# Last layer's second feed-forward product: channels on the partitions before, tokens on the partitions after

## The chip, the cores and the metric

One Trainium2 chip, one of its cores, one launch. The metric is device time in microseconds (us) of the whole program. Before the change the median of three timed runs is 2346.48 us (2346.24 to 2348.11).

## What is computed

A backbone of two layers over 256 latent tokens with 256 context tokens ahead of them, 1024 channels wide. Each layer mixes the tokens in three branches (a state-space scan, grouped attention, differential attention), adds the result to the stream and normalises it, and then runs a gated feed-forward product of inner width 2816 and normalises again. In the last layer only the latent tokens are wanted (`need_ctx` is false). What the change touches is the end of that layer:

```python
def swiglu(h, w_in, w_out):
    a, b = jnp.split(h @ w_in, 2, axis=-1)
    return (jax.nn.silu(a) * b) @ w_out
...
x = layer_norm(DEEPNORM_ALPHA * x + mod_l[5][:, None]
               * swiglu(modulate(x, mod_l[3], mod_l[4]), ffn_w_in[i], ffn_w_out[i]),
               ln2_g[i], ln2_b[i])
...
return x
```

`mod_l` is a row of six times 1024 modulation values, made from the condition vector by one product with `ada_w[i]` (1024 x 6144) and the bias `ada_b[i]`; its sixth part, `mod_l[5]`, is the gate of the feed-forward product.

## The kernel before

The program is not run in the order in which it is written. `trunk` calls a recorder (`Plan`), which notes each instruction with its tiles; `Plan.schedule` then orders all of it with a list schedule for the whole program. It has a price for each instruction (`Plan.cost`), slots for the tiles of each class (`SIZES`: 65 buffers of 128x512 in class `s2`, 15 of 128x1024 for weights in `w4`, 8 PSUM banks in `ps`), and a priority that says when TensorE, never idle, would want a result. So a change of a price or of a tile's life can move instructions anywhere in the program. All instructions are emitted from one line (L586 before, L585 after); in the trace, groups are told apart by tile names and shapes: `s` is a 128x512 buffer, `shared` a part of one, `w` a weight tile, `ps` a PSUM bank, `cst` and `id` constants, `tiny` small columns, `misc` parameter columns.

fp32 weights are split on chip: ScalarE copies the rounded high part (type fp32r), VectorE subtracts to get the low part (`load_w`). A product is then three fp32r matmuls, high x high, high x low and low x high (`dense`, `mm3`). Products that stay in fp32 run in two records each in the trace; transposes run in one.

The end of the last layer before the change, in the order of recording:

- `w_o` product, 8 blocks of 128 channels; its result plus the residual `xa` goes to `rt`. Then `make_ada(i, range(10, 12))`: the product for the last two blocks of modulation values, 16 matmuls that run four side by side on strips of the array (a strip operation), then a copy, four transposes and a reduction to columns.
- `segment`: the layer norm of `rt` (`layer_norm`, channels on the partitions, so the sums over channels are products with a block of ones) and the next stream `hT`. `late` writes the residual for the next norm to DRAM (`xd1`), in steps during the first blocks; `load_xa` reads it back.
- Feed-forward: 22 blocks of 128 inner channels in three batches (8, 8, 6). A block is two products of 24 matmuls with 256 columns (`psd` banks, at most six), then sigmoid, two multiplications and `split` into `hh`, `hl`. After each batch the second product: for each of 8 blocks of output channels one load of `ffn_w_out` (128 x 1024, or 768 in the last batch) and 24 (18) matmuls with 256 columns (the tokens), then `resid`, which multiplies by the gate and adds to `rt2`.
- `layer_norm` of `rt2`, eight multiplications and activations with scale and bias, 16 transposes back to token rows, four copies, four loads of 256 KB to `out`.

PE, VectorE (DVE) and ScalarE (ACT) take their instructions in emitted order. Loads go out on SyncE's queue (SP), some on GpSimd's (POOL).

Of the kernel before, what the change touches and what calls it, by code (L numbers as in the profile page):

```python
# [10 lines left out]
F32R = mybir.dt.float32r  # L11
AF = mybir.ActivationFunctionType
ALU = mybir.AluOpType
# [31 lines left out]
LAST_ADA = 2  # L45
# [31 lines left out]
class View:  # L77
    """A slice of a planned tile: which part of it (for dependencies) and how to reach it."""
# [108 lines left out]
class Plan:  # L187
    """Records the program, then orders it with a list schedule that knows the on-chip memory."""
# [19 lines left out]
    def cost(self, eng, fn, out, ins, kw):  # L208
# [3 lines left out]
        if eng == "PE":  # L212
            if fn == "transpose":
                return 109
            rhs, m = ins[1], ins[0].shape[-1]
            n = self.free(rhs)
            if rhs.dt() == F32R:
                return max(n / 2.4 if n >= 256 else 4 * n / 2.4, 107) + 2.5
            return 2 * max(2 * n / 2.4, 107) + 4
        if eng == "DVE":  # L220
# [3 lines left out]
            if fn == "tensor_reduce":  # L224
# [89 lines left out]
    def schedule(self):  # L314
        """The best of some rounds: after each, what the tensor engine waited for gets a higher priority."""
# [30 lines left out]
    def round(self, bump):  # L346
# [13 lines left out]
        # priority: when the tensor engine, never idle, would want the result, and not long after the program's order  # L360
# [47 lines left out]
        def place(b):  # L408
            """The slot (and the part of it) that a tile goes to: one in part use before an empty one."""
# [197 lines left out]
def trunk(tc, x, c, cx, c_ctx, ada_w, ada_b, w_in, b_gate, conv_w, conv_b, dt_bias, a_log, ssm_d, norm_w,  # L607
# [42 lines left out]
    def load_w(src, kt, cols, step=0):  # L650
# [3 lines left out]
        if step:  # L654
            # columns in the order (halves, axes) instead of (axes, halves)
# [121 lines left out]

    def ada_parts(i, ccs, tag="aw"):
        """Modulation columns of some blocks of 512: each block has rows of its own in every strip of one sum."""
# [3 lines left out]
        for m, cc in enumerate(ccs):  # L783
            for k0 in (0, 4):
                ws = [t2(tag=tag, cap=CAP[tag]) for _ in range(4)]
                for g in range(4):
                    S.dma_start(out=ws[g], in_=ada_w[i][(k0 + g) * 128:(k0 + g + 1) * 128, cc * 512:(cc + 1) * 512])
                with plan.strips():
                    for g in range(4):
                        T.matmul(ps[32 * g:32 * g + 32, :], scT[:, k0 + g, 30 - 2 * m:62 - 2 * m], ws[g],  # L790
# [819 lines left out]
```

## Time and profile before

| what | value |
|---|---|
| median of the timed runs | 2346.48 us |
| span of the profiled execution (the program on the core, first to last instruction) | 2345.3 us |
| PE busy | 2301.0 us, 98% of the span |
| VectorE, ScalarE busy | 1670.1 us (71%), 1422.4 us (61%) |
| DMA, mean over the span | 158 GB/s |

No other time of the profiled execution is given; the median of the runs lies 1.2 us over its span. How to read it: PE is the engine that the others serve. A stretch in which PE is busy throughout lasts as long as its matmuls take; where it is not, something else sets the time. PE's busy time is made of modelled ends, so the pace of matmuls is taken from their count in a stretch.

### The profile page before, as it was taken

What the parts mean: (1) busy time and instruction counts of PE and PEld (TensorE: products, weight loads), DVE (VectorE), ACT (ScalarE), POOL (GpSimd) and SP (SyncE); (2) the same over time, 40 slices, a digit from 0 to 9 for tenths busy, and PEclk for the clock granted to TensorE, in tenths of its full rate; (3) what the DMA queues carried; (4) which work ended last, traced back from release to release, by engine and by line L of the source; (5) the groups of instructions that cost most, each with busy time, mean ns of one, the idle gap of its engine ahead of it and who ended that gap; (6) DMA issues with size and microseconds to landing.
All of it is one profiled execution on the core that took longest, in us unless ns stands there. A gap on an engine that the chain in (4) does not pass through costs nothing. (4 is left out here: it accounts for less than half of the span.)

```text
span 2345.3 us, 38903 instructions
## 1 busy us (share of the span) xinstructions
PE 2301.0 (98%) x14423; PEld 1940.3 (83%) x14423; DVE 1670.1 (71%) x3438; ACT 1422.4 (61%) x2887; POOL 135.1 (6%) x216
## 2 busy tenths in 40 slices
PE   8999999999999999999999999999999999999998
PEld 4877777887887788898777778989988798998997
DVE  3889857888988864476333337999698888767655
ACT  4778745867767753345323235888586676646554
POOL 3102102000100100000000000001010100000000
PEclk9999999999999999999999999999999999999998
DMA  9746544332433465576555425527443345798662
GB/s 332 214 135 175 181 132 135 102 112 72 133 104 98 133 216 175 184 219 213 171 163 168 139 74 151 150 76 217 132 129 114 105 126 164 214 274 240 191 188 66
DMA packets 520702, 370.37 MB, mean 158 GB/s; under 512 B 20706, under 2 KB 472674, under 8 KB 520512
## 3 DMA queue, kind: packets, MB, share of 16 engines
q1 hardware_dynamic: 507296, 329.63, 47.3%
q0 software_dynamic: 13216, 38.25, 5.5%
q8 instruction: 113, 1.85, 0.3%
q14 instruction: 77, 0.63, 0.1%
HBM read 334.00 MB, written 33.82 MB: 157 GB/s over the span
## 5 line engine op out<-in xcount | busy, mean ns | idle before, releaser
L586 PE MATMUL ps<-s,w 128*128 128x512 f32 (+2 forms) x7608 | 1524.0, 355 | 8.2 <-DVE s L586 4.6
L586 PEld LDWEIGHTS ps<-s,w 128*128 128x128 f32 (+1 forms) x7608 | 1236.0, 189 | 237.1 <-issue 28.8
L586 ACT CAST w<-w 128x1024 fp32r<-128x1024 f32 (+2 forms) x486 | 454.4, 944 | 486.3 <-DVE w L586 256.8
L586 DVE TENSOR_TENSOR w<-w,w 128x1024 fp32r<-128x1024 f32 (+2 forms) x486 | 528.0, 1092 | 299.8 <-PE ps L586 203.0
L586 PE MATMUL ps<-shared,w 128*128 128x256 f32 x2544 | 313.2, 283 | 0.0
L586 PE MATMUL ps<-s,s 128*64 128x128 f32 (+6 forms) x2320 | 303.2, 361 | 7.6 <-DVE s L586 2.1
L586 PEld LDWEIGHTS ps<-shared,w 128*128 128x128 f32 x2544 | 308.5, 192 | 0.5 <-issue 0.3
L586 ACT ACTIVATE s<-s 128x512 f32<-128x512 f32 x424 | 260.6, 630 | 31.0 <-DVE s L586 24.7
L586 PEld LDWEIGHTS ps<-s,s 128*64 128x64 f32 (+3 forms) x2320 | 186.9, 152 | 90.6 <-issue 31.9
L586 DVE TENSOR_TENSOR s<-s,s 128x512 f32<-128x512 f32 (+2 forms) x298 | 196.2, 674 | 36.7 <-ACT s L586 34.5
L586 DVE TENSOR_TENSOR s<-s,ps 128x512 f32<-128x512 f32 x116 | 79.1, 684 | 133.3 <-PE ps L586 65.7
L586 DVE SCALAR_TENSOR_TENSOR s<-ps,misc,s 128x510 f32<-128x510 f32 (+2 forms) x188 | 139.3, 741 | 13.9 <-ACT s L586 11.8
L586 PE MATMUL ps<-w,s 128*128 128x256 f32 x960 | 119.7, 284 | 0.0
L586 PEld LDWEIGHTS ps<-w,s 128*128 128x128 f32 x960 | 117.2, 192 | 2.2 <-issue 1.5
L586 DVE TENSOR_TENSOR shared<-shared,shared 128x256 f32<-128x256 f32 (+2 forms) x241 | 97.2, 417 | 24.4 <-ACT shared L586 22.6
L586 DVE TENSOR_TENSOR s<-ps,s 128x256 fp32r<-128x256 f32 (+1 forms) x204 | 85.6, 444 | 30.4 <-ACT s L586 25.7
L586 ACT ACTIVATE shared<-shared 128x256 f32<-128x256 f32 x232 | 92.4, 416 | 23.4 <-DVE shared L586 20.7
L586 ACT CAST s<-ps 128x256 fp32r<-128x256 f32 (+1 forms) x204 | 74.4, 396 | 36.0 <-PE ps L586 32.1
L586 ACT ACTIVATE s<-ps,misc 128x512 f32<-128x512 f32 x68 | 50.6, 744 | 73.2 <-PE ps L586 73.0
L586 POOL DMA_DIRECT2D s<-dram x96 | 71.9, 753 | 375.0 <-PE ps L586 274.7
L586 ACT ACTIVATE s<-ps,tiny 128x512 f32<-128x512 f32 x112 | 76.7, 689 | 26.5 <-DVE tiny L586 18.9
L586 DVE SCALAR_TENSOR_TENSOR shared<-ps,misc,shared 128x256 f32<-128x256 f32 (+2 forms) x144 | 67.2, 478 | 29.4 <-PE ps L586 20.4
(102 smaller groups left out, 1512.5 us busy)
## 6 DMA issues: line engine op xcount, KB each, us to landing
w<-in_w_in_dram SPq DMA_DIRECT2D x200, 512.0 KB, 4.0
s<-in_ada_w_dram SPq DMA_DIRECT2D x192, 256.0 KB, 4.9
w<-in_ffn_w_in_dram SPq DMA_DIRECT2D x88, 512.0 KB, 3.9
s<-dram POOLq DMA_DIRECT2D x96, 256.0 KB, 5.6
s<-dram SPq DMA_DIRECT2D x64, 256.0 KB, 4.1
w<-in_w_ssm_out_dram SPq DMA_DIRECT2D x32, 512.0 KB, 4.1
w<-in_ffn_w_out_dram SPq DMA_DIRECT2D x32, 512.0 KB, 3.9
shared<-dram SPq DMA_DIRECT2D x112, 128.0 KB, 3.9
```

The costliest lines, as they stand in the source:

```text
L586: getattr(attr[op.eng], fn)(*[real(v) for v in args], **{a: real(v) for a, v in kw.items()})
```

## The change

The last layer gets a second half of its own, `last_ffn`; the loop with three batches stays for the first layer alone.

- The second product is turned round: 128 tokens of `hh` or `hl` are the stationary operand and 512 output channels of `ffn_w_out` rows the moving one. Four PSUM banks (two halves of the tokens, two halves of the channels) collect the whole product from block 0 to block 21. Each block is multiplied as soon as it is made, those of blocks 18 to 21 together at the end, first all of token half 0, then all of token half 1.
- The gate is needed as rows in place of columns: `gate_rows` runs the same strip product, copies it, and with two fp32 matmuls by a selecting matrix puts the sums on all partitions, where the bias (a row loaded to all partitions) is added. The four transposes and the reduction go.
- The residual is turned to token rows on chip (`token_resids`, 16 transposes, in `xres`) in place of the way through DRAM.
- The norm works along the free dimension with `bn_stats` and `bn_aggr`; `ln2_g` and `ln2_b` are loaded as rows to all partitions, four loads of 256 KB on POOL's queue beside two for the bias. The final transposes go.
- `Plan.cost` prices an fp32r matmul anew. `LAST_ADA` is gone with the same value, 2, written out. Comments in the code go too.

```diff
             if rhs.dt() == F32R:
-                return max(n / 2.4 if n >= 256 else 4 * n / 2.4, 107) + 2.5
+                return (n if n >= 256 else 4 * n) / 2.4 + m / 9.6
...
+            def token_resids():
+                for q in range(2):
+                    xo = []
+                    for d in range(4 * q, 4 * q + 4):
+                        xo.append(t1())
+                        V.tensor_tensor(xo[-1], rt[d, 256], rss[0][1], ALU.mult)
+                        A.activation(xo[-1], xo[-1], AF.Identity, scale=ac[:, 0, d:d + 1], bias=ac[:, 1, d:d + 1])
+                    yield
+                    for t in range(2):
+                        ps = psum()
+                        for j in range(4):
+                            transpose(ps[:, j * 128:(j + 1) * 128], xo[j][:, t * 128:(t + 1) * 128])
+                        xres[t, q] = t2()
+                        A.copy(xres[t, q], ps)
+                    yield
...
+        def gate_rows():
+            bias = []
+            for m in range(2):
+                bias.append(t2())
+                src = ada_b[i][5 * D + m * 512:5 * D + m * 512 + 512]
+                G.dma_start(out=bias[m], in_=src.unsqueeze(0).to_broadcast([128, 512]))
+            ps = psum("ada", CAP["ada"])
+            for m in range(2):
+                for _ in ada_terms(i, ps, m, 10 + m, m == 0, m == 1):
+                    pass
+            ev = t2()
+            A.copy(ev, ps)
+            for m in range(2):
...
+                psg = psum()
+                T.matmul(psg, sel, ev, start=True, stop=True)
+                V.tensor_tensor(bias[m], bias[m], psg, ALU.add)
+            return bias
+
+        def last_ffn(grow):
+            outs = {(t, q): psum() for t in range(2) for q in range(2)}
+            waiting = []
+            for j in range(22):
...
+                split(hh, hl, sg)
+                wh, wl = load_w(ffn_w_out[i][j * 128:(j + 1) * 128, :], 1, D)
+                for t in range(2):
+                    waiting.append((t, j, hh, hl, wh, wl))
+                if j < 18 or j == 21:
+                    waiting.sort(key=lambda v: v[0])
+                    for t, n, hh, hl, wh, wl in waiting:
+                        ts_ = slice(t * 128, t * 128 + 128)
+                        for q in range(2):
+                            qs = slice(q * 512, q * 512 + 512)
+                            mm3(outs[t, q], hh[:, ts_], hl[:, ts_], wh[:, 0, qs], wl[:, 0, qs], n == 0, n == 21)
+                    waiting = []
...
+            for t in range(2):
+                st, mv, rs = tiny(12), tiny(2), tiny(1)
+                for q in range(2):
+                    r = xres[t, q]
+                    gated = t2()
+                    V.tensor_tensor(gated, outs[t, q], grow[q], ALU.mult)
+                    V.tensor_tensor(r, r, gated, ALU.add)
+                    V.bn_stats(out=st[:, 6 * q:6 * q + 6], in_=r)
+                V.bn_aggr(out=mv, in_=st.rearrange("p (c s) -> p c s", s=6))
+                rsqrt(rs, mv[:, 1:2], 1)
+                for q in range(2):
+                    r = xres[t, q]
+                    V.scalar_tensor_tensor(r, r, mv[:, 0:1], gb[0, q], ALU.subtract, ALU.mult)
+                    V.scalar_tensor_tensor(r, r, rs, gb[1, q], ALU.mult, ALU.add)
+                    S.dma_start(out=out[0, t * 128:(t + 1) * 128, q * 512:(q + 1) * 512], in_=r)
...
-            if i > 0 and LAST_ADA:
-                make_ada(i, range(12 - LAST_ADA, 12))
+            if not need_ctx:
+                grow = gate_rows()
             segment(t0, r)
```

The order moves everywhere in the program; three places matter below. A row names the written tile, the tiles read and the size of the result.

PE, second product of the last layer. Before, the end of one block of 128 output channels in the last batch (`ps_24818`), with 256 tokens as columns:

```order
L586 MATMUL ps_24818<-shared_3_24717,w_4703_24704 128x256 x2
L586 MATMUL ps_24818<-shared_28_24361,w_4704_24715 128x256
L586 MATMUL ps_24818<-shared_39_24438,w_4704_24715 128x256
L586 MATMUL ps_24818<-shared_30_24505,w_4704_24715 128x256
L586 MATMUL ps_24818<-shared_22_24573,w_4704_24715 128x256
L586 MATMUL ps_24818<-shared_28_24647,w_4704_24715 128x256
L586 MATMUL ps_24818<-shared_3_24717,w_4704_24715 128x256
```

After, the last six of token half 0 (banks `ps_22749`, `ps_22754`) and the first three of token half 1 (`ps_22760`); 21 more in the last two banks follow and end the program's matmuls:

```order
L585 MATMUL ps_22749<-w_4688_24477,shared_70_24549 128x512
L585 MATMUL ps_22749<-w_4689_24491,shared_70_24549 128x512
L585 MATMUL ps_22749<-w_4688_24477,shared_70_24549 128x512
L585 MATMUL ps_22754<-w_4688_24477,shared_70_24549 128x512
L585 MATMUL ps_22754<-w_4689_24491,shared_70_24549 128x512
L585 MATMUL ps_22754<-w_4688_24477,shared_70_24549 128x512
L585 MATMUL ps_22760<-w_4646_24205,shared_18_24358 128x512
L585 MATMUL ps_22760<-w_4647_24246,shared_18_24358 128x512
L585 MATMUL ps_22760<-w_4646_24205,shared_18_24358 128x512
```

The matmuls of the norm and the 16 transposes that stood behind the second product are gone from there: the last matmul of the program is one of the product.

VectorE, the end of the program. Before, from the last block's `resid` on (what follows it is the norm, with PE and ScalarE between):

```order
L586 SCALAR_TENSOR_TENSOR shared_50_22480<-ps_24860,misc_12157,shared_50_22480 128x256
L586 TENSOR_TENSOR shared_16_21337<-shared_16_21337,shared_50_22480 128x256
L586 SCALAR_TENSOR_TENSOR shared_49_23274<-ps_24883,shared_49_23274 128x256
L586 SCALAR_TENSOR_TENSOR shared_28_23341<-ps_24883,shared_28_23341 128x256
...
L586 TENSOR_TENSOR shared_50_22480<-shared_50_22480,shared_4_24891 128x256 x2
L586 COPY s_4729_24942<-ps_24924 128x512
L586 COPY s_4733_24959<-ps_24944 128x512
```

After, token half 1 whole; the eleventh operation of half 0 stands among them:

```order
L585 TENSOR_TENSOR s_4698_24614<-ps_22760,s_4310_443 128x512
L585 TENSOR_TENSOR s_4699_24617<-ps_22765,s_4311_453 128x512
L585 TENSOR_TENSOR s_4383_22756<-s_4383_22756,s_4698_24614 128x512
L585 TENSOR_TENSOR s_4405_22845<-s_4405_22845,s_4699_24617 128x512
L585 BN_STATS tiny_24621<-s_4383_22756 128x6
L585 BN_STATS tiny_24621<-s_4405_22845 128x6
L585 SCALAR_TENSOR_TENSOR s_4403_22839<-s_4403_22839,tiny_24601,s_4619_487 128x512
L585 BN_AGGR tiny_24625<-tiny_24621 128x2
L585 SCALAR_TENSOR_TENSOR s_4383_22756<-s_4383_22756,tiny_24625,s_4616_465 128x512
L585 SCALAR_TENSOR_TENSOR s_4405_22845<-s_4405_22845,tiny_24625,s_4617_475 128x512
L585 SCALAR_TENSOR_TENSOR s_4383_22756<-s_4383_22756,tiny_24629,s_4618_481 128x512
L585 SCALAR_TENSOR_TENSOR s_4405_22845<-s_4405_22845,tiny_24629,s_4619_487 128x512
```

All that follows the last matmul is on VectorE now, but for two small activations and the stores; ten operations of half 0 stand ahead of these rows.

POOL's queue in the opening of the program. Before, the parameter loads of layer 1 are followed by the first store of a later stage:

```order
L586 DMA shared_1_207<-in_diff_lambda_dram 1x16x16
L586 DMA tiny_403<-in_ssm_a_log_dram 64x1 x2
L586 DMA tiny_403<-in_ssm_dt_bias_dram 64x1 x2
L586 DMA dram_861<-s_162_847 64x512
L586 DMA s_448_929<-dram_861 128x4x128
```

After, the six row loads of the last layer stand between them:

```order
L585 DMA tiny_407<-in_ssm_a_log_dram 64x1 x2
L585 DMA tiny_407<-in_ssm_dt_bias_dram 64x1 x2
L585 DMA s_4310_443<-in_ada_b_dram 128x512
L585 DMA s_4311_453<-in_ada_b_dram 128x512
L585 DMA s_4616_465<-in_ln_g_dram 128x512
L585 DMA s_4617_475<-in_ln_g_dram 128x512
L585 DMA s_4618_481<-in_ln_b_dram 128x512
L585 DMA s_4619_487<-in_ln_b_dram 128x512
L585 DMA dram_888<-s_162_877 64x512
```

The scheduler puts them at the start of the program, so six of the 65 buffers of class `s2` hold them from there to the last layer's end.

## Rows read from the trace of the kernel before

**Rows 1.** The page: busy time and share of the span; 40 equal slices.

```profile
PE 2301.0 (98%) x14423; PEld 1940.3 (83%) x14423; DVE 1670.1 (71%) x3438; ACT 1422.4 (61%) x2887; POOL 135.1 (6%) x216
...
PE   8999999999999999999999999999999999999998
```

**Rows 2.** Busy time by stretch: engines (x instructions), PE clock, DMA share, GB/s.

```profile
0.00:200.00 200.00, 186.75 (x1165) 138.70 (x1166) 144.30 (x382) 134.46 (x303) 34.20 (x62) 0.97 0.70 216
200.00:800.00 600.00, 594.91 (x3368) 473.21 (x3368) 487.20 (x1136) 414.12 (x940) 55.75 (x84) 1.00 0.43 125
800.00:1400.00 600.00, 600.00 (x3059) 487.77 (x3055) 299.29 (x448) 247.50 (x360) 2.95 (x5) 1.00 0.56 171
1400.00:2100.00 700.00, 690.73 (x4988) 622.19 (x4988) 587.63 (x1230) 501.03 (x1077) 42.22 (x65) 1.00 0.54 154
2134.00:2325.90 191.90, 191.22 (x1590) 190.57 (x1588) 123.42 (x186) 102.73 (x167) 0.00 (x0) 1.00 0.58 168
2325.90:2345.30 19.40, 8.08 (x37) 3.93 (x36) 7.80 (x20) 9.10 (x21) 0.00 (x0) 0.68 0.15 54
```

**Rows 3.** The same view, two stretches with matmuls of one kind each.

```profile
880.00:1000.00 120.00, 120.00 (x531) 99.38 (x530) 52.19 (x59) 43.70 (x55) 0.00 (x0) 1.00 0.58 179
2200.00:2300.00 100.00, 100.00 (x836) 100.00 (x835) 60.66 (x81) 53.41 (x83) 0.00 (x0) 1.00 0.62 179
```

**Rows 4.** PE's instructions in order of time: start us, us, what.

```profile
1701.07 2.35 PE L586 MATMUL ps<-id,s 128*128 128x128 f32 x20
1703.34 0.96 PE L586 MATMUL ps<-s,shared 64*128 64x512 f32 x6
1704.35 5.42 PE L586 MATMUL ps<-s,s 128*128 128x512 f32 x12
...
2012.40 1.35 PE L586 MATMUL ps<-shared,w 128*128 128x256 f32 x10
2013.67 1.53 PE L586 MATMUL ps<-s,s 128*64 128x128 f32 x24
2015.13 1.93 PE L586 MATMUL ps<-shared,w 128*128 128x256 f32 x14
2016.90 0.28 PE L586 MATMUL ps<-s,w 128*128 128x256 f32 x1
```

**Rows 5.** All engines in order of time at the end of the program.

```profile
2299.82 26.08 PE L586 MATMUL ps<-shared,w 128*128 128x256 f32 x216
...
2325.94 0.48 DVE L586 SCALAR_TENSOR_TENSOR shared<-ps,misc,shared 128x256 f32<-128x256 f32 x1 [1.21 <-PE ps L586]
2326.46 0.42 DVE L586 TENSOR_TENSOR shared<-shared,shared 128x256 f32<-128x256 f32 x1
2326.94 0.70 PE L586 MATMUL ps<-shared,cst 128*128 128x256 f32 x2 [1.03 <-DVE shared L586]
...
2335.84 4.09 PE L586 MATMUL ps<-id,shared 128*128 128x128 f32 x16 [2.11 <-ACT shared L586]
...
2338.55 2.87 SPq L586 DMA_DIRECT2D out_dram<-s  x4
...
2339.97 0.59 ACT L586 COPY s<-ps 128x512 f32<-128x512 f32 x1 [0.27 <-PE ps L586]
```

**Rows 6.** Groups by shape, VectorE and ScalarE: count, busy us, mean ns, idle before.

```profile
L586 DVE TENSOR_TENSOR s<-s,s 128x512 f32<-128x512 f32 x224 | 149.8, 684 | 14.7 <-ACT s L586 13.3
L586 DVE TENSOR_REDUCE tiny<-ps 128x1 f32<-128x512 f32 x96 | 63.1, 680 | 1.1 <-PE ps L586 0.8
L586 DVE SCALAR_TENSOR_TENSOR s<-s,tiny,s 128x512 f32<-128x512 f32 x32 | 23.8, 742 | 0.0
L586 DVE TENSOR_SCALAR tiny<-tiny 128x1 f32<-128x1 f32 x144 | 19.7, 142 | 0.0
L586 ACT ACTIVATE tiny<-tiny 128x1 f32<-128x1 f32 x2 | 0.4, 201 | 0.0
```

**Rows 7.** VectorE in order of time, four operations back to back.

```profile
1702.78 2.48 DVE L586 TENSOR_TENSOR s<-s,shared 128x512 f32<-128x512 f32 x4
```

**Rows 8.** The opening: stretches as in rows 2, and POOL in order of time.

```profile
30.00:40.00 10.00, 10.00 (x57) 7.23 (x61) 3.27 (x9) 1.17 (x4) 1.92 (x4) 0.88 1.05 381
60.00:70.00 10.00, 10.00 (x85) 8.43 (x85) 8.40 (x23) 4.76 (x10) 0.00 (x0) 1.00 1.03 345
70.00:80.00 10.00, 10.00 (x90) 9.41 (x89) 8.28 (x16) 5.30 (x10) 3.70 (x6) 1.00 0.60 148
...
30.89 1.03 POOL L586 DMA_DIRECT2D tiny<-in_ssm_dt_bias_dram  x2
72.86 0.53 POOL L586 DMA_DIRECT2D dram<-s  x1 [40.94 <-DVE s L586]
```

More of the change, by code (lines that the diff above doesn't have):

```diff
@@ L776, in load_scalars, with ada_terms @@
         lam[i] = nl
+    def ada_terms(i, ps, m, cc, first, last, tag="aw"):
+        for k0 in (0, 4):
+            ws = [t2(tag=tag, cap=CAP[tag]) for _ in range(4)]
+            for g in range(4):
+                S.dma_start(out=ws[g], in_=ada_w[i][(k0 + g) * 128:(k0 + g + 1) * 128, cc * 512:(cc + 1) * 512])
+            with plan.strips():
+                for g in range(4):
+                    T.matmul(ps[32 * g:32 * g + 32, :], scT[:, k0 + g, 30 - 2 * m:62 - 2 * m], ws[g],
+                             start=(first and k0 == 0), stop=(last and k0 == 4), tile_position=(0, 32 * g))
+            yield
     def ada_parts(i, ccs, tag="aw"):
@@ L783, in ada_parts @@
         for m, cc in enumerate(ccs):
[L784 to L790, printed above, removed]
-                                 start=(m + k0 == 0), stop=(cc == ccs[-1] and k0 == 4), tile_position=(0, 32 * g))
-                yield
+            yield from ada_terms(i, ps, m, cc, m == 0, cc == ccs[-1], tag)
         ev = t2()
@@ L1473, in trunk @@
                 resid(rt[d, t0], d, ps[:, 0:256], xa, 2, r)
-            if i > 0 and LAST_ADA:
-                make_ada(i, range(12 - LAST_ADA, 12))
+            if not need_ctx:
+                grow = gate_rows()
             segment(t0, r)
         def next_ada():
-            for ccs in (range(4), range(4, 12 - LAST_ADA)):
+            for ccs in (range(4), range(4, 10)):
                 yield from ada_parts(i + 1, ccs)
+        if not need_ctx:
+            last_ffn(grow)
+            continue
         rt2 = {(d, t0): t1() for t0, _ in segs for d in range(KT)}
-        if need_ctx:
-            load_bias(i + 1)
-            load_params(i + 1)
-            load_scalars(i + 1)
-        adas = next_ada() if need_ctx else iter(())
+        load_bias(i + 1)
+        load_params(i + 1)
+        load_scalars(i + 1)
+        adas = next_ada()
         for j0, j1 in ((0, 8), (8, 16), (16, 22)):
@@ L1530, in trunk @@
                         resid(rt2[d, t0], d, ps[:, t0 - T0:t0 - T0 + 256], prev, 5, r)
-                if need_ctx and j1 == 22:
+                if j1 == 22:
                     segment(*part[0])
-        if not need_ctx:
-            rs = layer_norm(rt2, 256)
-            for d in range(KT):
-                o = rt2[d, 256]
-                V.tensor_tensor(o, o, rs, ALU.mult)
-                A.activation(o, o, AF.Identity, scale=P[:, C_G2 + d:C_G2 + d + 1], bias=P[:, C_B2 + d:C_B2 + d + 1])
-            for q in range(2):
-                for t in range(2):
-                    ps = psum()
-                    for j in range(4):
-                        transpose(ps[:, j * 128:(j + 1) * 128], rt2[4 * q + j, 256][:, t * 128:(t + 1) * 128])
-                    ot = t2()
-                    (A.copy if t else V.tensor_copy)(ot, ps)
-                    S.dma_start(out=out[0, t * 128:(t + 1) * 128, q * 512:(q + 1) * 512], in_=ot)
     order = plan.schedule()
```

34 lines of the change are left out of this document (29 added, 5 removed).

## The prediction

> **What bounds the kernel now.** I read the page first. PE is busy 98% of the span, VectorE 71%, ScalarE 61% [rows 1], so a saving counts only where it shortens PE's work or the time in which PE has nothing to do. The stretches say where that is: 13.2 us idle in the first 200 us, 5.1 us between 200 and 800, nothing from 800 to 1400, 9.3 us from 1400 to 2100, under 1 us in the last layer's feed-forward part (2134 to 2325.9), and in the last 19.4 us PE is a helper of the norm [rows 2]. So there are two separate places: a feed-forward stretch in which each matmul counts at full length, and a tail in which PE's work is nearly without meaning and a chain of VectorE, ScalarE and PE sets the time.
>
> The pace of matmuls comes from counts. A stretch with fp32r matmuls of 512 columns alone does 531 in 120 us, 0.226 us each; one with 256 columns does 836 in 100 us, 0.1196 us each [rows 3]. So 512 columns cost less than twice 256.
>
> The tail: the long run of matmuls ends at 2299.82 + 26.08 = 2325.90, VectorE takes the last result at 2325.94, the norm goes round PE, ScalarE and VectorE until 2335.84, when the 16 transposes begin; the last copy ends at 2339.97 + 0.59 = 2340.56, and the program at 2345.3 [rows 5]. That is 19.4 us after the last product, of which 4.74 us lie behind the last copy (the store).
>
> **The change part by part.** All is summed against the profiled execution (span 2345.3 us; the median of the runs is 1.2 us longer) and then put on the median.
>
> *The second product.* Before, 22 blocks x 8 channel blocks x 3 = 528 matmuls with 256 columns; after, 22 x 4 x 3 = 264 with 512. 528 x 0.1196 = 63.1 us; 264 x 0.226 = 59.7 us [rows 3]. The stretch is PE bound [rows 2], so this is -3.5 us on the path. The Trainium skill (TensorE: Matmul & The Clock Gate, section Back-to-back issue gap) gives a warm gap of N / 2.4 + 2.5 ns; by it the two would cost 57.7 and 57.0 us and the saving would be 0.7 us. The rows have about 13 ns beyond N / 2.4 for either width, not 2.5; the rows decide here, and the rule is a rival below.
>
> *Moved to PE's busy part.* The 16 transposes of the residual now stand among the matmuls of the feed-forward part: 20 took 2.35 us with their last one's end, the next work starting 2.27 us after the first [rows 4], so 0.11 us each and +1.8 us. The two fp32 products that spread the gate have 512 columns: six of them, two records each, took 5.42 us, the following work starting 5.35 us after the first [rows 4], 0.87 us each at most, +1.7 us. Four transposes of the modulation columns go, -0.4 us. The strip products stay. So PE's body changes by -3.5 + 1.8 + 1.7 - 0.4 = -0.4 us.
>
> *The tail.* Call E the end of the last matmul. Token half 0 has its last one 24 x 0.226 = 5.4 us before E, so its chain runs under the matmuls of half 1. A VectorE operation on 512 elements lasts 0.68 us, with two inputs and a column 0.74 us [rows 6]; back to back the starts lie (2.48 - 0.68) / 3 = 0.60 us apart [rows 7], and 0.66 us for the longer form by the same overlap. `bn_stats` is not in this trace; the nearest row is the reduction over 512 elements at 0.68 us [rows 6], so I take 0.60 as well. `bn_aggr` I take as a small operation, 0.15 us (0.142) [rows 6].
> Half 0: first multiplication at E - 6.1, the second (it must wait for its bank) at E - 5.4, two additions and two `bn_stats` until E - 2.3, `bn_aggr` until E - 2.1, two subtractions with scale until E - 0.7, one of the two last steps until E - 0.1. ScalarE's two steps of 0.2 us [rows 6] lie under the subtractions.
> Half 1: six operations from E - 0.1 at 0.60 us until E + 3.5, the left-over step of half 0 until E + 4.2, `bn_aggr` until E + 4.3, two subtractions until E + 5.7, the last two steps until E + 7.1. Then the store, 4.74 us as now [rows 5]: E + 11.8. Against 19.4 us that is -7.6 us. Nothing hides in this chain, so its bounds count in full: with `bn_stats` at the 0.40 us spacing of a cheaper form, -8.4; at twice 0.60, 2.4 us more in all four, -5.2.
>
> *The price of a matmul in the scheduler.* Every stretch gets another order. In it PE changes from fp32r to fp32 181 times; before 165. What such a visit costs: 24 records of fp32 took 1.46 us from 2013.67 to the next kind at 2015.13, and the matmuls after it come 14 in 1.77 us, where 14 x 0.1196 is 1.67 [rows 3, 4]. Against the 0.109 us that two such records cost in a long stretch (0.11 us per transpose is the same pass) this is some 0.15 + 0.1 us, with the 0.07 us that the ten matmuls ahead took too long, 0.3 us a visit. 16 more are +4.8 us at most; where a visit stands in a wait it costs nothing, 0. I take +2.
>
> *The opening.* Six loads of 256 KB now stand at about 31 us in POOL's queue, which then had nothing to do until 72.86 [rows 8]. The DMA is full there (share 1.05 and 1.03, 345 to 381 GB/s), with slack from 70 us on [rows 8]. 1.57 MB at 355 GB/s are 4.4 us for whoever is behind them; PE was busy throughout both full stretches shown, out of loads that had come earlier, so 0 is the other end. I take +1. Nothing waits on POOL's queue in that time.
>
> *What costs nothing.* The stores and loads of the residual through DRAM go and rows of 4 KB come for `ffn_w_out`; DMA is at 0.58 there [rows 2]. VectorE and ScalarE are busy 61% and 53% of that stretch [rows 3], and the change takes about as much from them as it adds, so PE covers them. `token_resids` adds eight pairs of small operations that were there before too.
>
> Sum: -0.4 - 7.6 + 2 + 1 = -5.0 us, so 2346.5 - 5.0 = 2341.5 us.
>
> **The rivals.** *The order is better.* The new price is nearly what rows 3 show (its formula gives 227 and 120 ns for 512 and 256 columns, the rows 226 and 119.6; the old one gave 216 and 109), so the scheduler sees PE's needs as late as they are. PE's idle time outside opening and tail is 5.1 + 9.3 = 14.4 us [rows 2]; half of it back gives 2334.3. For it: those are waits for VectorE and ScalarE, which an order can mend. Against: it is an order made around 6 buffers fewer.
>
> *Buffers.* This is the case on the slow side. Six of 65 buffers are held by rows from the opening to the end. In the crowded stretches (200 to 800, 1400 to 2100), where a tile must wait for a free buffer, loads and results come later, and PE, last in the chain, waits. Price: the idle time of these stretches once more, +14.4 us, 2355.9. It makes the change slower by our bound once it passes 9.7 us. For it: these are the stretches in which PE idles now. Against: 594.91 of 600 us busy leaves little sign of want [rows 2].
>
> *The loads and visits at full price.* Opening +4.4, visits +4.8: 2347.7, and the gain is gone.
>
> *Four banks.* With four banks held, a block's two products and the next block's share the other four. A bank comes back after about four products' time, 24 x 0.1196 = 2.9 us each, and the chain that frees it is some 3 us, so it decides only if that chain takes over 8 us. If each of 22 blocks waited 0.3 us: +6.6, 2348.1. Little speaks for it.
>
> *Equal pace.* If a matmul followed the rule of the skill above, the product would save 0.7 instead of 3.5 us: 2344.3. Rows 3 speak against it.
>
> *It does not do what it says* is no case apart: the order shows the new tail as written.
>
> **How the numbers follow.** A measurement of this kernel can tell some 0.2% from no change, 4.7 us: faster is under 2341.8, slower over 2351.2. The forecast gets 0.52; its own spread is 2336 to 2347, from the bounds of tail, visits and opening and some of the order, and its centre lies just under the line, so 0.28 of it counts as faster and 0.24 as the same. Better order 0.16, faster. Loads and visits at full price 0.11, four banks 0.03, equal pace 0.02, all the same. Buffers 0.16, slower. Together 0.44 faster, 0.40 the same, 0.16 slower. The range: 2333, just under the better order, up to 2351, which leaves out most of the buffers' case.
>
> **What would show it.** From the last matmul to the end 11.8 us (11.0 to 14.2), nearly all VectorE with the store behind it, and no PE in it. In the feed-forward part 12 matmuls of 512 columns in about 2.7 us per block, PE without waits. `bn_stats` at 0.6 to 0.7 us. In the opening, PE's work in the first 100 us a few us behind. Idle time of PE in 200 to 800 and 1400 to 2100 as now, 14 us. It would be wrong if that idle time differs by more than 5 us (order or buffers), or if the last layer's stretch has waits for banks.

## Result and profile after

The changed kernel took 2400.72 us (2396.6 to 2404.92) against 2346.36 us (2344.41 to 2348.11) of the kernel before: ratio 1.0231, 95% interval 1.0216 to 1.0245. Forecast were 2341.5 us and a range from 2333 to 2351. The profiled execution has a span of 2403.2 us against 2345.3 us; it is the longest of the four runs of this kernel.

The page of the kernel after, its busy times and two lines of its 40 slices, answers to [rows 1]:

```profile
PE 2322.8 (97%) x14139; PEld 1932.7 (80%) x14139; DVE 1675.1 (70%) x3413; ACT 1420.6 (59%) x2872; POOL 137.8 (6%) x222
...
PE   7999999999999989999999999999999999999998
...
PEclk8999999999999989999999999999999999999999
```

PE idles 80.4 us (span less busy time) where it idled 44.3, and is busy 21.8 us longer though it has 284 instructions fewer. The stretches of the kernel after, columns as in [rows 2], say where:

```profile
0.00:100.00 100.00, 82.65 (x464) 55.18 (x465) 47.27 (x132) 46.25 (x91) 27.86 (x53) 0.90 0.91 287
100.00:200.00 100.00, 98.44 (x592) 79.22 (x591) 83.74 (x206) 73.78 (x171) 5.87 (x10) 0.98 0.39 120
200.00:800.00 600.00, 580.68 (x3254) 453.82 (x3253) 470.01 (x1101) 400.91 (x911) 49.67 (x76) 0.99 0.41 118
800.00:1400.00 600.00, 589.64 (x3020) 477.06 (x3020) 314.35 (x496) 255.75 (x400) 12.47 (x18) 0.99 0.58 178
1400.00:2100.00 700.00, 683.64 (x4694) 598.40 (x4693) 570.04 (x1203) 488.82 (x1052) 39.78 (x61) 1.00 0.47 133
```

Idle in 200 to 800 are 19.3 us (5.1 before), in 800 to 1400 10.4 (0), in 1400 to 2100 16.4 (9.3), in the first 200 us 18.9 (13.2) [rows 2]. Of what the change rewrites, only the last layer's early row loads and selectors run there; the rest is code that both kernels have. The waits of PE in the kernel after (us in total, times, longest) name VectorE and ScalarE, busy 70% and 59% of the span; 5.7 us in all are for transfers:

```profile
PE ps L585 <- DVE s L585: 37.7, 37, 5.6
PE ps L585 <- ACT shared L585: 13.2, 17, 2.4
PE ps L585 <- ACT s L585: 7.9, 12, 2.1
```

These two engines in their turn stand for stores more than they did. The largest such waits:

```profile
ACT s L585 <- DMA dram<-s: 9.6, 3, 7.2
ACT shared L585 <- DMA dram<-shared: 9.1, 7, 2.7
DVE s L585 <- DMA dram<-s: 7.8, 2, 6.8
```

With the smaller ones they are 32.6 us, against 2.0 before. A store reads the buffer that it writes out, so this is what a want of buffers would look like; the profile names the store and not the reason.

The new form of the last layer's second half, on the other hand, runs as forecast. First PE's instructions in order of time in the feed-forward part of the last layer, then all engines at the end of the program (it answers to [rows 5]):

```profile
2241.34 5.92 PE L585 MATMUL ps<-shared,w 128*128 128x256 f32 x48
2247.09 2.89 PE L585 MATMUL ps<-w,shared 128*128 128x512 f32 x12
2249.82 5.92 PE L585 MATMUL ps<-shared,w 128*128 128x256 f32 x48
2255.57 2.90 PE L585 MATMUL ps<-w,shared 128*128 128x512 f32 x12
```

```profile
2387.69 4.92 PE L585 MATMUL ps<-w,shared 128*128 128x512 f32 x21
...
2390.33 0.21 DVE L585 BATCH_NORM_AGGREGATE tiny<-tiny 128x2 f32<-128x12 f32 x1
...
2392.58 1.28 DVE L585 TENSOR_TENSOR s<-ps,s 128x512 f32<-128x512 f32 x2
...
2393.78 1.28 DVE L585 TENSOR_TENSOR s<-s,s 128x512 f32<-128x512 f32 x2
2394.98 1.28 DVE L585 BATCH_NORM_STATS2 tiny<-s 128x6 f32<-128x512 f32 x2
...
2397.06 2.74 DVE L585 SCALAR_TENSOR_TENSOR s<-s,tiny,s 128x512 f32<-128x512 f32 x4
```

Twelve matmuls of 512 columns take 2.73 us from start to start (2247.09 to 2249.82). The last matmul ends at 2392.61, VectorE at 2399.80, the program at 2403.2: 10.6 us where there were 19.4. So the loss lies ahead of the last layer's feed-forward part, nearly all of it in code that is the same in both kernels but stands in another order.

To follow it, one mark is used below: the start of the 10000th fp32r matmul, counted in PE's order. It lies in the last layer, ahead of its feed-forward part, and all kernels have the same fp32r work up to there. Before: 2068.2 us, and 277.1 from there to the end. After: 2135.0, and 268.2.

### The profile page after: what moved, and what is told of

Same layout as the page of the kernel before. It is cut to its first block, busy times and chain, and to the rows that moved or that the text cites. A ratio compares the mean times of both kernels' runs of the same rounds, so it can differ in the third digit from the quotient of the medians.

```text
span 2403.2 us, 38382 instructions
## 1 busy us (share of the span) xinstructions
PE 2322.8 (97%) x14139; PEld 1932.7 (80%) x14139; DVE 1675.1 (70%) x3413; ACT 1420.6 (59%) x2872; POOL 137.8 (6%) x222
## 4 chain that ended last, share of the span: by engine, by line
PE 73%; DVE 7%; issue 7%; DMA 6%; ACT 6%; POOL 1%; SPq 0%; DVEq 0%; POOLq 0%; ACTq 0%
PE ps L585 73%; DVE s L585 4%; ACT s L585 3%; ACT shared L585 2%; DVE shared L585 1%; DMA s<-dram 1%; DMA dram<-shared 1%; DMA shared<-dram 1%; DMA s<-in_ada_w_dram 1%; DVE tiny L585 1%; DVE w L585 1%; ACT w L585 1%; SPq L585 0%; DMA s<-in_x_dram 0%; POOL s L585 0%
## 5 line engine op out<-in xcount | busy, mean ns | idle before, releaser
L585 PE MATMUL ps<-s,w 128*128 128x512 f32 (+2 forms) x7608 | 1524.9, 356 | 12.6 <-DVE s L585 10.2
L585 PE MATMUL ps<-s,s 128*64 128x128 f32 (+6 forms) x2320 | 316.1, 369 | 29.2 <-DVE s L585 20.9
L585 PE MATMUL ps<-shared,w 128*128 128x256 f32 x2016 | 253.7, 284 | 4.2 <-ACT shared L585 4.2
L585 PEld LDWEIGHTS ps<-shared,w 128*128 128x128 f32 x2016 | 247.3, 192 | 9.0 <-ACT shared L585 5.7
L585 DVE TENSOR_TENSOR s<-ps,s 128x256 fp32r<-128x256 f32 (+2 forms) x208 | 88.7, 449 | 30.9 <-ACT s L585 21.3
L585 DVE TENSOR_TENSOR shared<-shared,shared 128x256 f32<-128x256 f32 (+2 forms) x221 | 89.1, 418 | 28.1 <-ACT shared L585 25.3
L585 ACT ACTIVATE s<-ps,tiny 128x512 f32<-128x512 f32 x112 | 76.4, 685 | 30.0 <-DVE tiny L585 21.8
L585 PE MATMUL ps<-id,s 128*128 128x128 f32 (+1 forms) x480 | 73.1, 285 | 11.4 <-DVE s L585 5.1
L585 DVE TENSOR_REDUCE tiny<-ps 128x1 f32<-128x512 f32 (+1 forms) x144 | 81.7, 593 | 1.8 <-PE ps L585 1.5
```

The costliest lines, as they stand in the source:

```text
L585: getattr(attr[op.eng], fn)(*[real(v) for v in args], **{a: real(v) for a, v in kw.items()})
```

## Experiments

Three suspects: the new **price** in `Plan.cost`, by which the schedule and the mix of the streams are made; things of the last layer that have no late input and so are placed **early**, at the opening, holding buffers to the end; and the **last layer's form** itself. Times are medians. Each is compared with runs of the kernel before on the same chip beside it: 2347.62 us for the first four experiments, 2346.51 for the buffers, the two uses of the price and 1 ns more, 2346.08 for 1 ns less, the 12 rounds and the rows behind a value, 2347.2 for the three with everything late, 2346.15 for the split of the 1 ns. Between these groups the kernel before differs by 1.5 us, so differences across groups are no finer than that. "Clock" in the expectations is the list schedule's own running time, not TensorE's clock.

### Price and rows, each alone and together

The changed kernel with the old price:

```diff
-                return (n if n >= 256 else 4 * n) / 2.4 + m / 9.6
+                return max(n / 2.4 if n >= 256 else 4 * n / 2.4, 107) + 2.5
```

> After with the old price of an fp32r matmul in the scheduler; the six row loads still stand in the opening. Theory P (the new price makes the worse order): about 2342 us, PE's idle time in 200 to 1000 us back to some 5 us. Theory R (six buffers held by rows from the opening on, and 1.5 MB of loads there): about 2400, as after. If both share it, between.

Measured 2375.77, ratio 1.0117 (1.0102 to 1.0132). 25 us of the loss go with the price; 28 stay.

The changed kernel with the new price, its six rows in the group of buffers (`aw`) that the modulation's weights pass through, so that they come behind those weights:

```diff
-            for m in range(2):
-                bias.append(t2())
...
+            for m in range(2):
+                bias.append(t2(tag="aw", cap=CAP["aw"]))
...
-                            gb[m, q] = t2()
+                            gb[m, q] = t2(tag="aw", cap=CAP["aw"])
```

> After with the new price, but the six rows in buffers of the modulation weights' group and loaded after these weights, so that their loads stand at the end of POOL's queue and no buffer is held early. Theory R: about 2341 us, the opening as before and PE's idle time in 200 to 1000 us some 5 us. Theory P: about 2400, as after.

Measured 2393.0, ratio 1.0193 (1.0176 to 1.021): late rows alone give back 8 us.

Both edits together:

> After with the old price and the late rows. Theories P and R both say about 2340 us, 6 us under before, by the shorter tail. If the last layer's new form itself costs the time (theory L): 2390 or more, with the loss behind 2130 us.

Measured 2352.72, ratio 1.0025 (1.0015 to 1.0034). So, as made late here, the rows cost 23 us at the old price and 8 at the new one, the price 40 without early rows and 25 with them: both are real, and they don't add. And 5 us over before remain where a gain was expected.

The kernel before with the new price line alone:

> Before with nothing but the new price of an fp32r matmul. Theory P: 2390 to 2400 us, the loss spread over the program's first half. Theory R: 2346, within 5 us of before, either way.

Measured 2384.24, ratio 1.0159 (1.0144 to 1.0174). The price alone, with nothing else of the change, costs 36.6 us, a little less than the 2390 to 2400 that its theory wanted. Stretches of this kernel:

```profile
0.00:100.00 100.00, 84.56 (x507) 59.52 (x508) 53.38 (x149) 53.77 (x115) 24.50 (x47) 0.93 0.91 283
...
200.00:800.00 600.00, 586.62 (x3305) 460.22 (x3302) 475.38 (x1118) 407.23 (x929) 54.26 (x82) 0.99 0.42 121
...
1400.00:2100.00 700.00, 680.26 (x4770) 601.66 (x4769) 575.74 (x1216) 494.15 (x1064) 41.97 (x65) 1.00 0.50 140
```

Idle 13.4 us in 200 to 800 and 19.7 in 1400 to 2100, against 5.1 and 9.3 [rows 2]: the same crowded stretches, by the order alone.

### Buffers without loads

The kernel before with six buffers fewer:

```diff
-SIZES = {"cst": 1, "id": 1, "w4": 15, "s2": 65, "misc": 4, "tiny": 40, "ps": 8}
+SIZES = {"cst": 1, "id": 1, "w4": 15, "s2": 59, "misc": 4, "tiny": 40, "ps": 8}
```

> The kernel before with six of its 65 buffers of 2 KB (the pool named s2) taken away, and nothing else: no early row loads, the old price, the old last layer. The early rows had cost 23 us at the old price (2375.8 against 2352.7 us) and 8 at the new one. If they cost that because six buffers are held from the opening to the last layer, this kernel loses the same without a single load: 2362 to 2372 us, its added waits of TensorE spread over the body as in the kernel with the old price and early rows (7 us in 100-300, 16 in 800-900). If they cost it because six loads of 256 KB stand among the opening's loads, this kernel is within 3 us of 2346.5 and waits as the kernel before does.

Measured 2373.39, ratio 1.0109 (1.0091 to 1.0128): +26.9 us without a single early load, slightly over the range expected. Its stretches:

```profile
0.00:200.00 200.00, 183.53 (x1106) 136.37 (x1106) 135.78 (x352) 122.36 (x269) 30.52 (x57) 0.98 0.66 201
200.00:800.00 600.00, 587.65 (x3307) 463.62 (x3306) 477.61 (x1110) 409.94 (x923) 50.24 (x77) 0.99 0.42 122
800.00:1400.00 600.00, 597.16 (x3080) 482.79 (x3079) 311.42 (x483) 257.71 (x399) 11.92 (x17) 1.00 0.57 177
```

Idle in 200 to 800 rises from 5.1 to 12.4 us. This is the rival "buffers", and it holds: 65 buffers are not slack, though PE was busy 594.91 of 600 us with them. How much of the 26.9 us any other new order would have cost is not told by this run alone; the order's own part is looked at below.

### By which of its uses the price acts

The price goes into the durations of the list schedule, and into `plan.spent`, the amounts by which the streams are mixed when the program is written down. The kernel before with the new price in the second use alone:

```diff
-            self.spent["PE"] += dur
+            n, m = self.free(ins[1]), ins[0].shape[-1]
+            new = fn == "matmul" and ins[1].dt() == F32R and not more
+            self.spent["PE"] += (n if n >= 256 else 4 * n) / 2.4 + m / 9.6 if new else dur
```

> The kernel before, in which the new price of a fp32r matmul goes only into the amount of work that the streams are counted by when the program is written down (plan.spent, which RATIO is held against); the list schedule keeps the old durations. The new price in both places cost the kernel before 36.6 us. If it acts by the mix in which the streams are written down: 2375 to 2390 us, here. If it acts by the list schedule's clock: 2347, within 5 us, here, and all of it in the next kernel.

Measured 2369.29, ratio 1.0093 (1.0078 to 1.0108), between the two forecasts.

And in the durations alone (the new line in `Plan.cost`, the old one for `spent`):

```diff
-                return max(n / 2.4 if n >= 256 else 4 * n / 2.4, 107) + 2.5
+                return (n if n >= 256 else 4 * n) / 2.4 + m / 9.6
...
+            self.spent["PE"] += max(n / 2.4 if n >= 256 else 4 * n / 2.4, 107) + 2.5 if old else dur
```

> The kernel before, in which the new price goes only into the durations that the list schedule works with (start and end of every matmul, and the priorities); the streams are mixed by the old price. If the price acts by the list schedule's clock: 2375 to 2390 us, with TensorE's waits at the opening, in 200-300, 700-800 and 1400-1800 as when both are new. If it acts by the mix: 2347 within 5 us.

Measured 2382.52, ratio 1.0145 (1.0129 to 1.0162). Either use alone costs (+22.8, +36.0), and both together no more than the second. Neither of the two theories, as written, is right alone.

### How fine the order is tuned

The kernel before, 1 ns more per fp32r matmul:

```diff
-                return max(n / 2.4 if n >= 256 else 4 * n / 2.4, 107) + 2.5
+                return max(n / 2.4 if n >= 256 else 4 * n / 2.4, 107) + 3.5
```

> The kernel before with every fp32r matmul priced 1 ns higher (110.5 for 109.5 ns at 256 columns), a tenth of what the new price adds there (120.0). It asks how much any new order costs, whatever its reason. If the loss grows with the price: +3 to +4 us, 2350. If every new draw of the schedule costs, since the order of before is a lucky one among many: as much as the new price itself, 2360 to 2385. If small changes of the price leave the order nearly as it is: within 2 us.

Measured 2357.66, ratio 1.004 (1.0025 to 1.0055): +11.2 us for a tenth of the new price's step at 256 columns, which none of the three forecasts had.

1 ns less (`+ 1.5`):

> The kernel before with every fp32r matmul priced 1 ns lower (108.5 ns at 256 columns); 1 ns higher cost 11 us. If a higher price is bad by its direction (TensorE late in the plan, so that other engines' work is put off), a lower one gains or costs nothing: 2340 to 2347. If it is any new order that costs, whichever way the price goes: 2353 to 2370.

Measured 2363.18, ratio 1.0068 (1.0053 to 1.0083): +17.1 us. So the direction of the price is not what matters.

A new order at the old price, `ROUNDS` 12 for 4:

> The kernel before with 12 rounds of the list schedule where there were 4; prices, buffers and program unchanged. The planner keeps the round whose own estimate of the end is the earliest, so only the order of the instructions is new, and by that estimate it is 2.7 us better than the order of before. If the added microseconds of the runs so far come from the price and the buffers themselves, this kernel is at 2346 within 3 us. If the order of before is one that happens to run well, and any other one costs, it is 2355 to 2375 although nothing was priced or held differently.

Measured 2347.89, ratio 1.0005 (0.9996 to 1.0014): nothing. So not every other order costs.

The 1 ns split by its two uses, as above with `dur + 1` for `spent`, or `+ 3.5` for the durations:

> The kernel before with 1 ns more per fp32r matmul only in the work that the streams are counted by (spent); the list schedule's durations stay. 1 ns in both uses cost 11 us (2357.7). If the mix of the streams is what small changes upset: 2355 to 2362. If the clock is: within 3 us of 2346.5.

> The kernel before with 1 ns more per fp32r matmul only in the list schedule's durations; the streams are mixed as before. If the mix is what small changes upset, this is a redrawn order and no more: 2344 to 2350, as with 12 rounds. If the clock carries it: 2354 to 2362.

Measured 2357.53 and 2357.43, ratios 1.0046 (1.0029 to 1.0063) and 1.0045 (1.003 to 1.006). Both cost the whole 11 us by themselves. Every changed price costs 11 us or more, while a redraw by 12 rounds at the same price moved the time by +1.8 here, and by -5.9 and +1.4 for two kernels below. Why stays open. One rival is left by it: part of what any step away from the order of before costs, some 11 us, may be no more than leaving that order.

### Where the last layer's gain had gone

The changed kernel at the old price, rows kept late by a first column written from a late value:

```diff
                 bias.append(t2())
+                V.tensor_copy(bias[m][:, 0:1], rt[0, 256][:, 0:1])
...
                             gb[m, q] = t2()
+                            V.tensor_copy(gb[m, q][:, 0:1], sg[:, 0:1])
```

> The changed kernel at the old price, its six row tiles first written in one column from a value of the place where they are wanted (a residual of the last layer, a gate of its block 16), so that neither tile nor load can come early; they are no longer bound to the four strips' pool order, as in the kernel with late rows at the old price (2352.7 us), which loses 9 us at 2100-2200 where a product waits for its weights' split. If that loss comes from the rows' pool order: 2342 to 2346. If it is what a new order costs: 2350 to 2365, with the added waits in other places. In both cases 10.9 us from the last matmul to the end.

Measured 2344.97, ratio 0.9994 (0.9984 to 1.0004). Its mark lies at 2077.6, 9.4 us behind that of before, and 268.5 us remain: the way from the mark to the end is 8.6 us shorter, but PE comes to the mark late. What it has over the kernel with both edits lies, in the profiles, behind the mark (268.5 for 273.4), as was expected if the `aw` buffers had cost it there. Measured from this kernel, early rows at the old price cost 30.8 us (2375.77), and neither of the two has the order of before; six buffers without loads cost 26.9.

The kernel with both edits, 12 rounds:

> The kernel with late rows at the old price (2352.7 us), with 12 rounds of the list schedule instead of 4: the planner's own estimate is only 0.4 us better, so this is one more order of the same work with the same prices and buffers. If the order alone moves the time: anywhere from 2343 to 2370, more than 3 us from 2352.7. If the last layer's new form fixes it: 2352.7 within 3 us. In both cases 10.9 us from the last matmul to the end.

Measured 2346.81, ratio 1.0003 (0.9993 to 1.0012); mark at 2074.2, again late, and 272.2 to the end. It is 5.9 us under the same kernel with 4 rounds: equal work, prices and buffers, so here the order alone moved the time by that much, and a difference of 6 us between two kernels does not name its cause by its size.

What still stood early shows in VectorE's instructions of the kernel with the rows behind a value, in order of time, at its very start:

```profile
3.34 0.23 DVE L585 TENSOR_REDUCE tiny<-id 128x1 f32<-128x4 f32 x2 [1.95 <-DMA id<-in_consts_dram]
3.54 0.36 DVE L585 COPY shared<-tiny 128x128 f32<-128x128 f32 x2
```

These are the two selectors of `gate_rows`, read some 2140 us later. They depend on a constant alone. With one more line they are late too:

```diff
                 pick, sel = tiny(1), th()
+                V.tensor_copy(pick, rt[0, 256][:, 0:1])
                 V.tensor_reduce(pick, ident.rearrange("p (g r) -> p r g", g=4)[:, 2 * m, :], AX.X, ALU.add)
```

> The kernel with the rows behind a value at the old price (2345.0 us), with the two selectors of the gate row made late as well (each pick is first written from a residual of the last layer). Nothing of the last layer can then be placed at the opening. If the selectors, held from the opening on, cost the 6 to 9 us up to the last layer: that point is reached as before (2068 us at the 10000th fp32r matmul, within 2) and the end comes 8 to 10 us earlier than before, 2336 to 2339 us. If the last layer's new form itself makes TensorE late ahead of it, or the gain is lost again behind it: 2344 to 2350.

Measured 2338.75, ratio 0.9963 (0.995 to 0.9975): 8.4 us faster than before, the best kernel here. VectorE and POOL in order of time, and the stretches:

```profile
2114.89 0.21 DVE L585 TENSOR_REDUCE tiny<-id 128x1 f32<-128x4 f32 x2
2116.11 0.35 DVE L585 COPY shared<-tiny 128x128 f32<-128x128 f32 x2
```

```profile
2117.52 1.18 POOL L585 DMA_DIRECT2D s<-in_ada_b_dram  x2 [66.97 <-DVE shared L585]
2282.96 1.13 POOL L585 DMA_DIRECT2D s<-in_ln_g_dram  x2 [164.27 <-DVE s L585]
```

```profile
0.00:200.00 200.00, 186.05 (x1164) 138.51 (x1165) 144.12 (x381) 134.33 (x302) 33.95 (x62) 0.97 0.70 216
200.00:800.00 600.00, 594.89 (x3363) 473.20 (x3361) 487.28 (x1136) 414.17 (x940) 55.62 (x84) 1.00 0.43 125
800.00:1400.00 600.00, 600.00 (x3059) 487.75 (x3059) 299.36 (x449) 247.83 (x361) 2.95 (x5) 1.00 0.55 171
1400.00:2100.00 700.00, 690.91 (x4990) 622.15 (x4989) 588.41 (x1230) 500.63 (x1077) 42.12 (x65) 1.00 0.53 154
```

These are the stretches of [rows 2] within 0.8 us. PE's first 12781 records in the trace are those of before, one by one in tile names and shapes, and so past the mark, which lies at 2068.4 (2068.2 before); 269.1 us remain for 277.1.

The same with the new price:

> The same with the new price. The price cost the kernel before 36.6 us (2384.2), and this kernel has that one's order up to the last layer. If the price and the early steps are separate causes: 2384 less the last layer's 8 to 10 us, 2373 to 2378, and the changed kernel's 2400.7 is then the price, +36, and the early rows and selectors, +23 to +27, less the last layer's gain. If the price hurts the new last layer as well: 2384 to 2395.

Measured 2382.77, ratio 1.0151 (1.0137 to 1.0165). Mark at 2113.6, 268.0 to the end. That is between the two forecasts. The price costs 44.0 us here. The way from the mark to the end is as long as at the old price, but the gain over the kernel before at this price is only 1.5 us: that one has its mark at 2109.7, and 272.4 to the end.

And with the old price and 12 rounds:

> The kernel with everything late at the old price, with 12 rounds of the list schedule instead of 4; by the planner's own estimate 3.3 us better than it. The kernel before went from 2346.1 to 2347.9 with 12 rounds. If the last layer's form is what gains: 2334 to 2341, below the kernel before by 6 us or more in this order too. If the gain hangs on one order: 2343 to 2350.

Measured 2340.1, ratio 0.9972 (0.9962 to 0.9983); mark at 2067.2, 269.7 to the end. So the gain shows in two orders.

The way from before to after in four steps, each between two measured kernels: last layer's form, all of it late, 2347.2 to 2338.75 (-8.4); the price, to 2382.77 (+44.0); the selectors early, to 2393.0 (+10.2; here the rows change their way of being late as well); the rows early, to 2400.72 (+7.7). Taken in another order the steps have other sizes (rows 23 or 30.8 at the old price); why they overlap was not shown. That price and rows are causes, and not only the leaving of a lucky order, rests on the pairs in which neither kernel has the order of before: price +40.3 (late rows) and +25.0 (early ones), rows +30.8 (old price).

| kernel | 3500th fp32r matmul starts | 10000th | span | mark to end |
|---|---|---|---|---|
| before | 853.4 | 2068.2 | 2345.3 | 277.1 |
| after | 911.2 | 2135.0 | 2403.2 | 268.2 |
| after, old price | 895.8 | 2109.5 | 2374.1 | 264.6 |
| after, late rows | 886.3 | 2115.6 | 2392.3 | 276.7 |
| both | 864.4 | 2077.0 | 2350.4 | 273.4 |
| rows behind a value | 864.1 | 2077.6 | 2346.1 | 268.5 |
| all late | 853.8 | 2068.4 | 2337.5 | 269.1 |
| all late, new price | 879.8 | 2113.6 | 2381.6 | 268.0 |
| before, new price | 881.4 | 2109.7 | 2382.1 | 272.4 |
| before, 59 buffers | 874.8 | 2096.0 | 2374.7 | 278.7 |

In every kernel that loses 20 us or more, over half of what it is late by at the 10000th matmul is there by the 3500th, in the first layer.

## Why the prediction was wrong

**The second product: right.** 12 matmuls of 512 columns in 2.73 us, 0.2275 us each (0.226 forecast), 48 of 256 in 5.75 us, 0.1198 each. By the gap that the Trainium skill (TensorE: Matmul & The Clock Gate, section Back-to-back issue gap) gives for an isolated matmul (the prediction left that word out), 12 of 512 columns would take 2.59 us as an estimate; the trace has 2.73, and the measurement decides.

**The tail: right in kind, a little shorter.** VectorE ends 7.2 us after the last matmul (7.1 forecast), `bn_stats` starts are 0.60 us apart and `bn_aggr` takes 0.21. Only the store was mis-sized: 3.4 us behind the last operation in place of 4.74. So 10.6 us against 11.8, just under the 11.0 that the prediction gave as its least. Body and tail of the last layer together were worth -8.0 in the sum; from the mark on it is 8.0 us in the profile of the kernel with everything late (277.1 to 269.1), and -8.4 in its median. That the sums agree to the tenth is in part luck: there the tail gains 8.9 us (10.5 for 19.4) where 7.6 were forecast, and the way from the mark to the last matmul of the product is 0.8 us longer (258.5 for 257.7) where the body was put at -0.4. Two slips of the working are too small to matter: six fp32 products in 5.35 us are 0.89 us each and not 0.87, and the 57.7 us are 57.6.

**"The price of a matmul in the scheduler": this step failed.** It counted 16 more visits of PE to fp32 work, at 0 to +4.8 us, and took +2. Measured on the kernel before alone it is +36.6. The order of that kernel has 175 such visits for 165, 3 us at the prediction's own 0.3 us each. What the runs show in place of the visits is more waiting and a longer busy time: in the profiles PE idles 18.5 us more (62.9 for 44.3) and is busy 18.3 us longer (2319.3 for 2301.0) with the same matmuls. The working priced the changes of kind that a new order makes PE execute, and not what it makes PE wait for; what the longer busy time consists of was not found. The prediction's own sign of being wrong came true as well: in 200 to 800 and 1400 to 2100 PE of the kernel after idles 35.7 us where 14 were expected. The rival "the order is better" held that a price nearer to the measured pace gives a better order. It is the reverse: 120 ns is what the rows show, and the kernel is faster with 109.5. In this scheduler the price acts as a knob, and not as a statement of the hardware: 1 ns either way costs 11 to 17 us. That its other knobs (the mix of the streams, the lead times) were set around the old price would explain it, but was not shown.

**"Buffers": the mechanism was right, its size and chance were not.** Six buffers cost 26.9 us, where the prediction had 14.4 us, the idle time of the crowded stretches once more. The argument against it, that 594.91 of 600 busy us leave little sign of want, was no evidence: with six buffers fewer the same stretch idles 12.4 us. Part of the loss is no idle time: with 59 buffers PE idles 15.6 us more and is busy 13.8 us longer.

**Not seen at all: the selectors.** The prediction counted the six rows as all that stands early. The order of the changed program has two reductions and two 128x128 copies at its start; making them late was worth 6.2 us (2344.97 to 2338.75) and brought back the order of before up to the mark. Whether by the tiles that they hold or by the other order that follows was not separated.

**The opening** was put at +1 (0 to 4.4), and this term too was too small. With early rows PE starts its 1000th record 10.0 us later at the new price (178.1 with late rows, 188.1 after) and 7.8 later at the old one (178.3, 186.1). At the new price that is as much as the early rows cost in all (7.7). One stretch shows it, first before, then after, with PE and VectorE of the kernel after in order of time and POOL's row loads:

```profile
50.00:60.00 10.00, 10.00 (x67) 8.57 (x66) 7.19 (x12) 8.56 (x18) 0.00 (x0) 1.00 1.14 316
50.00:60.00 10.00, 4.57 (x22) 2.11 (x17) 2.96 (x10) 5.19 (x11) 0.00 (x0) 0.84 1.06 303
```

```profile
53.49 1.08 PE L585 MATMUL ps<-s,w 128*64 128x512 f32 x4
59.32 0.76 DVE L585 TENSOR_TENSOR s<-shared,s 128x256 fp32r<-128x256 f32 x2 [6.76 <-DMA dram<-s]
60.14 7.27 PE L585 MATMUL ps<-s,w 128*64 128x512 f32 x20 [5.57 <-DVE s L585]
```

```profile
30.14 1.10 POOL L585 DMA_DIRECT2D s<-in_ada_b_dram  x2
31.22 1.06 POOL L585 DMA_DIRECT2D s<-in_ln_g_dram  x2
32.28 1.22 POOL L585 DMA_DIRECT2D s<-in_ln_b_dram  x2
85.43 0.54 POOL L585 DMA_DIRECT2D dram<-s  x1 [51.93 <-DVE s L585]
```

PE stands 5.57 us for VectorE, which stood 6.76 us for a store to end. Of the kernels looked at here (before, after, the first five experiments and everything late), only the two with early rows have a wait of VectorE for a store in the first 105 us (6.8 and 6.0 us); 59 buffers without the loads do not bring it. So it goes with loads and buffers together, and their shares in it were not separated. POOL's first store comes at 85.43 for 72.86 [rows 8].

**No waits for banks** in the last layer's feed-forward part: 48 and 12 matmuls alternate without a gap in the lines above, and from 2185 us to the last matmul PE waits 2.5 us in all, each time for ScalarE. That rival was rightly small.

## What to carry to other kernels

Where a planner orders the whole program, a change of one stage is two changes, and the second, the new order of all other stages, can be several times the first (here 8 us gained and over 60 lost): price it by trying the planner's edit alone on the old kernel. Look in the new order for steps without a late input (a constant selector, a row that is only loaded); this planner puts them at the start, where they hold buffers to the end, and a first write from a late value moves them. And a price nearer to one engine's measured pace need not give a better schedule: here it gave a worse one.

## What the runs showed of the hardware

A long wait of PE can cost more than its length. In the kernel after, PE's instructions and then the stretches around one:

```profile
863.51 0.66 PE L585 MATMUL ps<-s,s 128*64 128x128 f32 x8 [0.45 <-DVE s L585]
868.86 2.83 PE L585 MATMUL ps<-s,s 128*64 128x128 f32 x24 [4.69 <-DVE s L585]
```

```profile
860.00:870.00 10.00, 3.07 (x37) 2.39 (x38) 7.67 (x22) 8.53 (x24) 2.24 (x3) 0.88 0.63 169
870.00:880.00 10.00, 7.92 (x46) 5.23 (x43) 6.96 (x18) 7.64 (x15) 0.00 (x0) 0.50 0.01 2
880.00:890.00 10.00, 10.00 (x43) 8.20 (x42) 7.73 (x12) 6.86 (x11) 0.00 (x0) 0.94 0.56 182
```

After 6.9 idle us of ten the granted clock stands at 0.50, its lower level of 1.2 GHz, for the next ten, while PE works 7.92 of them, and at 0.94 in the ten after. Against the kernel with everything late at the old price, whose matmuls are the same, the kernel after idles 35.8 us longer (80.4 and 44.6) and is busy 29.9 us longer (2322.8 and 2292.9). The mean granted clock is 0.987 for 0.993, 0.013 of 2403.2 less 0.007 of 2337.5 or 15 us at most of that; the rest of the longer busy time was not itemised.
